# A decoder layer's last projection: eight feature blocks by seven quarter products, the residual through DRAM, one weight cast moved

## The chip, the core and the metric

The kernel runs on one core of a Trainium2 chip. The core has a matrix engine (TensorE, PE in the profile; PEld are its weight loads), VectorE (DVE), ScalarE (ACT), GpSimd (POOL) and SyncE (SP), which here issues the DMAs. Each engine works through its own instructions in order and waits on semaphores. The metric is the device time of one execution in microseconds. The kernel before took 1062.61 us (median of three runs, 1062.47 to 1064.94).

## What is computed

One decoder layer over 512 tokens of width 1024, all in float32. A token mixer (attention, pooling and a state-space scan) ends in a projection w_o that is added to the residual. The part that matters here comes after it:

```python
def rmsnorm(x, g):
    y = xf * lax.rsqrt(jnp.mean(xf * xf, axis=-1, keepdims=True) + NORM_EPS)
    return y * g

def conv_ffn(u, w_up, conv_w, conv_b, w_down):
    h = causal_dwconv(u @ w_up, conv_w, conv_b)      # 512 x 5632
    a, v = h[..., :D_FF], h[..., D_FF:]              # D_FF = 2816 = 22 x 128
    return (jax.nn.silu(a) * v) @ w_down             # 512 x 1024
...
x = x + merged @ w_o[i]
x = x + conv_ffn(rmsnorm(x, ln2_g[i]), ...)
return rmsnorm(x, final_g)
```

The last projection multiplies 512 x 2816 activations by the 2816 x 1024 matrix w_down. With features in 22 blocks of 128 (KF), tokens in four blocks of 128 and columns in two halves of 512, that is 22 x 4 x 2 = 176 block products.

## The kernel before

**A float32 product is three matmuls.** Each operand is split into a high part, rounded to the type that TensorE takes (float32r), and a low part, the rest. `mm3` (matmul at L221) adds high by high, high by low and low by high in one PSUM bank: over all feature blocks of a job first with the weight's high part, then high again, and only then with its low part.

**Weights come as jobs.** The program is a list of jobs, each with a piece of weights, mostly a tile of 128 partitions by 2048 elements (1 MB), and a body that issues its matmuls. The main loop gives each job n, before its body, a `prepare`: `low` of job n+1 (VectorE subtraction, L204), `cast` of job n+2 (ScalarE, two halves, L184), `fetch` of job n+3 (a DMA on SP, L174). Raw weights have two buffers, high parts three and low parts two, so a fetch waits until a low part has been taken, and a low part waits until TensorE has finished the job that had its buffer. The two halves of a cast are normally put in a list (`second`) and issued at the next calls of `step`, which also advances small pieces of other work (`running`).

**The order on TensorE, ScalarE, VectorE and GpSimd is that of the program text** (a schedule by hand). SP's order is found when the kernel is built, by a scheduler.

**The seam between w_o and up.** The w_o jobs run for token blocks 0 and 1, then 2 and 3, each with column half 0 and then 1. `wo_jobs` adds the result to the residual tiles X1 (L939), starts the norm with half 0 (`norm_early`: squares on ScalarE at L306, product with the gain on POOL at L330) and ends it with half 1 (`norm_late`, L306, then xg at L339, v, a root, and u at L347); the result is transposed on TensorE (`norm_turn`, L319) and split into uh and ul (L322, L323). For the last w_o job and the first up job `prepare` is called with `later=True` from the job's body, and returns a part that is run at a later place: for the last w_o job, after block 3's norm has been issued. An argument `now` says whether the cast is issued at once (last w_o job: yes) or with that part (first up job). The first two up jobs (`opening`, L1036) begin with the 256 tokens whose norm is done, and transpose blocks 2 and 3 between their products.

**The up projection.** 22 jobs of 256 columns; `up_evac` applies the convolution and gate (L1000, L1003, L1005, POOL at L1008) and `later` splits each of the 22 feature blocks in high and low (L1016, L1017), kept in ACTS.

**The down projection.** `down_jobs(0)` and `down_jobs(1)`, one per column half: six jobs each (four feature blocks a job, the last with two), 12 matmuls for each full job and token block, four accumulators. Results are added to X1 (L1078); half 0 starts the final norm, and half 1 ends it and stores the output (L1086). In half 1 the last two jobs run token block by token block, so that the norms follow one another.

Small tiles of 128 x 512 come from one pool of 54 slots (`T`); PSUM has four banks for `MM` and four for `SM`.

## Time and profile before

| what | value |
|---|---|
| median of three runs | 1062.61 us |
| profiled execution, time | 1064.09 us |
| its span, first to last instruction | 1062.2 us |
| mean granted TensorE clock | 0.995 |
| down projection on TensorE, 528 matmuls | 119.69 us |
| one 128x512 matmul in it | 0.2267 us |
| low part of a 128x2048 weight tile, VectorE | 2.29 us |
| cast of half of one, ScalarE | 1.04 us |
| bytes moved in the span | 115.50 MB |

The profile's page gives busy times of engines, the span in 40 slices, the chain of work that ended last, and groups of instructions with what ended the idle time before them. A row of a timeline has start, duration, engine, line, operation, output and inputs, and in brackets the idle time before and who ended it. Matmuls are pipelined, so their single durations (0.389 us) are longer than the step from one to the next; the step is the length of a stretch over its matmuls.

### The profile page before, as it was taken

The numbers are of one execution on the slowest core, as the hardware profiler recorded it, in microseconds if no ns is written. First come the engines' busy times: TensorE is split into PE (matmuls) and PEld (weight loads), VectorE is DVE, ScalarE is ACT, GpSimd is POOL, SyncE is SP. The second block draws the span as 40 slices with busy tenths as digits, with TensorE's granted clock in tenths as the row PEclk, the third lists the DMA queues.
The fourth block names the chain that finished last, engine by engine and source line by source line (L and its number), as shares of the span: only waits on it lengthen the run. The fifth ranks groups of instructions, "written<-read, shape, count | busy, mean of one in ns | idle before, by whom it ended". The sixth has DMA issues, their size and how long they took to land.

```text
span 1062.2 us, 13018 instructions
## 1 busy us (share of the span) xinstructions
PE 1045.9 (98%) x5268; PEld 874.4 (82%) x5268; DVE 576.8 (54%) x777; ACT 431.1 (41%) x698; POOL 135.1 (13%) x118
## 2 busy tenths in 40 slices
PE   8999999999999999999999999989999999999997
PEld 8878889888788887787888888888888888888885
DVE  5552523245667547667658766556656565532315
ACT  6343412232445633558536224534444444431311
POOL 1580000000000001100161500002111111110100
PEclk9999999999999999999999999989999999999999
DMA  7236233251221365442243337333232323232312
GB/s 237 79 115 179 82 100 107 72 140 50 83 80 60 83 166 158 110 129 81 80 111 119 119 97 263 119 118 101 95 104 81 118 80 119 80 119 69 110 60 79
DMA packets 116426, 115.50 MB, mean 109 GB/s; under 512 B 5235, under 2 KB 101302, under 8 KB 116367
## 3 DMA queue, kind: packets, MB, share of 16 engines
q1 hardware_dynamic: 116367, 114.68, 35.5%
q8 instruction: 41, 0.67, 0.3%
q14 instruction: 18, 0.15, 0.0%
HBM read 110.87 MB, written 2.22 MB: 106 GB/s over the span
## 4 chain that ended last, share of the span: by engine, by line
PE 91%; ACT 2%; issue 2%; DVE 2%; DMA 1%; POOL 0%; SPq 0%; DVEq 0%; ACTq 0%; POOLq 0%
PE pa L221 35%; PE pu L221 22%; PE pb L221 17%; PE pqk L221 9%; PE ps L512 1%; PE ppw L221 1%; PE po L551 1%; PE pt L539 1%; PE pu L1036 1%; ACT wh L184 1%; PE py L808 1%; DVE wl L204 1%; PE pyo L814 1%; DMA raw<-in_w_in_dram 1%; DMA raw<-in_ffn_w_up_dram 0%
## 5 line engine op out<-in xcount | busy, mean ns | idle before, releaser
L204 DVE TENSOR_TENSOR wl<-raw,wh 128x2048 fp32r<-128x2048 f32 (+3 forms) x94 | 219.2, 2333 | 137.9 <-PE pb L221 67.7
L184 ACT CAST wh<-raw 128x1024 fp32r<-128x1024 f32 (+2 forms) x186 | 187.2, 1025 | 109.6 <-PE pb L221 40.8
L221 PE MATMUL pa<-uh,wh 128*128 128x512 f32 x384 | 99.3, 400 | 0.3 <-ACT wh L184 0.3
L1003 DVE SCALAR_TENSOR_TENSOR hc<-pu,fcol,hc 128x510 f32<-128x510 f32 x88 | 65.9, 749 | 55.9 <-ACT hc L1000 54.3
L221 PE MATMUL pa<-ul,wh 128*128 128x512 f32 x384 | 95.0, 389 | 0.0
L221 PE MATMUL pa<-uh,wl 128*128 128x512 f32 x384 | 94.9, 389 | 0.0
L221 PEld LDWEIGHTS pa<-ul,wh 128*128 128x128 f32 x384 | 72.1, 188 | 15.3
L221 PEld LDWEIGHTS pa<-uh,wl 128*128 128x128 f32 x384 | 72.1, 188 | 15.0
L221 PE MATMUL pu<-ul,wh 128*128 128x512 f32 (+1 forms) x352 | 83.5, 379 | 0.0
L221 PE MATMUL pu<-uh,wl 128*128 128x512 f32 (+1 forms) x352 | 83.5, 379 | 0.0
L221 PE MATMUL pu<-uh,wh 128*128 128x512 f32 (+1 forms) x352 | 83.5, 379 | 0.0
L221 PEld LDWEIGHTS pa<-uh,wh 128*128 128x128 f32 x384 | 69.9, 188 | 16.5 <-issue 1.7
L221 PEld LDWEIGHTS pu<-uh,wl 128*128 128x128 f32 x352 | 64.2, 188 | 12.5
L221 PEld LDWEIGHTS pu<-ul,wh 128*128 128x128 f32 x352 | 64.2, 188 | 12.5
L221 PEld LDWEIGHTS pu<-uh,wh 128*128 128x128 f32 x352 | 64.1, 188 | 12.4
L1000 ACT ACTIVATE hc<-pu,fcol,fcol 128x512 f32<-128x512 f32 x40 | 31.2, 780 | 83.5 <-PE pu L221 83.5
L1008 POOL TENSOR_TENSOR hc<-hc 128x512 f32<-128x512 f32 x22 | 31.6, 1435 | 230.1 <-DVE hc L1003 188.1
L787 POOL TENSOR_TENSOR xd<-xc,dec 128x512 f32<-128x512 f32 x6 | 6.4, 1065 | 361.6 <-DVE xc L778 343.0
L533 ACT ACTIVATE sb<-sb,nm 128x128 f32<-128x128 f32 (+1 forms) x72 | 30.1, 419 | 46.9 <-DVE nm L530 33.2
L221 PE MATMUL pb<-wh,fh 128*128 128x512 f32 x176 | 47.7, 389 | 0.0
L221 PE MATMUL pb<-wl,fh 128*128 128x512 f32 x176 | 47.7, 389 | 0.0
L221 PE MATMUL pb<-wh,fl 128*128 128x512 f32 x176 | 47.7, 389 | 0.0
(273 smaller groups left out, 1601.8 us busy)
## 6 DMA issues: line engine op xcount, KB each, us to landing
raw<-in_w_in_dram SPq DMA_DIRECT2D x25, 1024.0 KB
raw<-in_ffn_w_up_dram SPq DMA_DIRECT2D x22, 1024.0 KB
raw<-in_w_in_dram SPq DMA_DIRECT2D x20, 512.0 KB
raw<-in_ffn_w_down_dram SPq DMA_DIRECT2D x10, 1024.0 KB
raw<-in_w_o_dram SPq DMA_DIRECT2D x8, 1024.0 KB
raw<-in_w_in_dram SPq DMA_DIRECT2D x6, 768.0 KB
raw<-in_w_b_dram SPq DMA_DIRECT2D x4, 1024.0 KB
al<-ad SPq DMA_DIRECT2D x16, 256.0 KB
```

The lines of the kernel that those rows point to most:

```text
L184: act.copy(job.high[:, :, o], job.raw[:, :, o])
L204: (eng or dve).tensor_tensor(l[:, :, o], job.raw[:, :, o], h[:, :, o].bitcast(F32), OP.subtract)
L221: pe.matmul(ps, l, r, start=first and n == 0, stop=last and n == total - 1)
L512: pe.matmul(pss[i][:, o:o + w * P], q[r, n * P:(n + 1) * P], k[r, kb * P:(kb + w) * P], start=True, stop=True)
L533: act.activation(sb[:, off:off + w * P], sb[:, off:off + w * P], AF.Exp, bias=nm[:, n, h:h + 1], accum_out=ls[:, n, h:h + 1])
L539: pe.transpose(pt[:, o:o + P], sb[:, o:o + P], eye)
L551: pe.matmul(po[DH * hh:DH * hh + DH, n * P:(n + 1) * P], V[g, kb + i][:, (2 * c + hh) * DH:(2 * c + hh + 1) * DH], probs[2 * c + hh, nb][: ...
L808: pe.matmul(py[DH * i:DH * i + DH, j * P:(j + 1) * P], xc[:, o:o + DH], als[j // 2][:, lo:lo + P], start=True, stop=True)
L814: pe.matmul(po[:, j * P:(j + 1) * P], prev[gi][:, j * P:(j + 1) * P], XS[10 + gi][:, cs], start=True, stop=True)
L1000: act.activation(t, ps, AF.Identity, bias=ff["c1"][:, ff["b"] + m:ff["b"] + m + 1], scale=fw(2, m))
L1003: dve.scalar_tensor_tensor(t[:, sh:], ps[:, :S - sh], fw(k, m), t[:, sh:], OP.mult, OP.add)
L1008: pool.tensor_tensor(a, a, t, OP.mult)
```

## The change

- **Seven products.** Of the 22 feature blocks the first eight (KS) are taken as four pairs. With tokens, features (even and odd blocks) and columns in halves, that part is a 2 x 2 by 2 x 2 product of quarters. It is computed by the scheme of seven products (Strassen's in Winograd's form) in place of eight, p1 to p7 of 24 matmuls each. `sums_of` forms the sums of activations in the up projection, `form` makes the differences of weights in place on VectorE, in buffers of one.raw, four.raw and in W. Four of the products go to PSUM banks of their own and are added to X1 by VectorE; p2, p4 and p3 share accumulators with the 14 other feature blocks, which `blocks_of` runs as before.
- **Order of the down jobs.** p2, four jobs of other blocks for half 0, p1, p5, p6, p7, p4, p3, four jobs for half 1.
- **The residual.** `put_x1` writes the eight X1 tiles to DRAM, `get_x1` reads them into one tile that takes the place of ul; W takes the place of uh.
- **The cast at the seam.** `prepare` has no `now`: with `later=True` low, cast and fetch are all in the part that is run later. For the last w_o job the cast moves behind block 3's norm; for the first up job nothing moves.

```diff
 DFF = 2816
 KF = DFF // P
+KS = 8
 C_Q, C_K, C_V = 0, AW, 2 * AW
 C_POOL = 3 * AW
...
     def fetch(job, cuts=1):
+        if job.load:
+            job.load()
+            return
...
     def cast(job, cuts=1, spread=False):
         w = job.c // cuts
+        if job.form:
+            job.raw = job.form()
         job.high = whp.tile([P, job.k, job.c], F32R, name="wh", tag="wh")
...
@@ -252,7 +260,7 @@
             wh, wl = ws
             mm3(acc[tb][:, :c], lambda k: wh[:, k - k0, :], lambda k: wl[:, k - k0, :],
                 lambda k: xh(k, tb), lambda k: xl(k, tb), range(k0, k1),
-                k0 == 0, k1 == nk, flip=True)
+                k0 == 0 and tb not in opened, k1 == nk and tb not in keep, flip=True)
...
@@ -260,7 +268,8 @@
             def body(ws, n=n, k0=k0, k1=k1):
                 if n == 0:
                     for tb in blocks:
-                        acc[tb] = (mk or MM)("pb")
+                        if tb not in opened:
+                            acc[tb] = (mk or MM)("pb")
...
                 for tb in blocks:
                     for a in (held if late else [(k0, k1, ws)]):
                         use(*a, tb)
-                    if k1 == nk:
+                    if k1 == nk and tb not in keep:
                         evac(tb, acc[tb])
                     if tb % 2:
                         step()
...
+    def put_x1():
+        nxt["x1"] = dram.tile([4, 2, P, S], F32, name="x1d")
+        for tb, h in X1:
+            sp.dma_start(nxt["x1"][tb, h], X1[tb, h])
+    def get_x1():
+        back = upool.tile([P, KD, S], F32, name="x1b", tag="ul")
+        for h in range(2):
+            for tb in range(4):
+                X1[tb, h] = back[:, 2 * tb + h, :]
+                sp.dma_start(X1[tb, h], nxt["x1"][tb, h])
...
@@ -1010,14 +1031,157 @@
         def later():
             yield
             k = m - KF
+            if k >= KS or k % 2:
+                h, l = T("fh", F32R), T("fl", F32R)
+                act.copy(h, a)
+                dve.tensor_sub(l, a, h.bitcast(F32))
+                ACTS[k] = (h, l)
+                if k < KS:
+                    yield
+                    for _ in sums_of(k // 2, HC[k - 1], a):
+                        yield
+                return
             if k == 0:
-                wide.extend(ypool.tile([P, 4, S], F32R, name=n, tag="xs") for n in ("fh", "fl"))
-            h, l = (t[:, k, :] for t in wide) if k < 4 else (T("fh", F32R), T("fl", F32R))
-            act.copy(h, a)
-            dve.tensor_sub(l, a, h.bitcast(F32))
-            ACTS[k] = (h, l)
+                wide.extend(ypool.tile([P, 4, S], F32R, name=n, tag="xs") for n in ("sh", "sl"))
+            t = T("f0", F32R)
+            act.copy(t[:, :256], a[:, :256])
+            dve.tensor_sub(t[:, 256:], a[:, :256], t[:, :256].bitcast(F32))
+            FS[0, k // 2] = (t[:, :256], t[:, 256:])
         running.append(later())
+    FS = {}
+    def sums_of(p, f0, f1):
+        lo, hi = slice(0, 256), slice(256, S)
+        sa, sb = T("sa"), T("sb")
+        dve.tensor_tensor(sa[:, lo], f0[:, hi], f1[:, hi], OP.add)
+        dve.tensor_tensor(sa[:, hi], sa[:, lo], f0[:, lo], OP.subtract)
+        dve.tensor_tensor(sb[:, lo], f0[:, lo], f0[:, hi], OP.subtract)
+        dve.tensor_tensor(sb[:, hi], f1[:, lo], sa[:, hi], OP.subtract)
+        yield
+        ah, al = (t[:, p, :] for t in wide)
+        bh, bl = T("sbh", F32R), T("sbl", F32R)
+        act.copy(ah, sa)
+        act.copy(bh, sb)
+        yield
+        dve.tensor_sub(al, sa, ah.bitcast(F32))
+        dve.tensor_sub(bl, sb, bh.bitcast(F32))
+        FS[1, p], FS[2, p] = (ah[:, lo], al[:, lo]), (ah[:, hi], al[:, hi])
+        FS[3, p], FS[4, p] = (bh[:, lo], bl[:, lo]), (bh[:, hi], bl[:, hi])
+    def down():
+        n2 = KS // 2
+        quarter = lambda two, h: w_down[:KS * P, h * S:(h + 1) * S].rearrange(
+            "(k two p) c -> two p k c", two=2, p=P)[two]
+        W, acc, rs = {}, {0: {}, 1: {}}, {}
+        def load(at, two, h):
+            def fn():
+                if not W:
+                    W["u"] = upool.tile([P, KD, S], F32, name="w3", tag="uh")
+                W[at] = W["u"][:, 4 * at:4 * at + 4, :]
+                sp.dma_start(W[at], quarter(two, h))
+            return fn
+        def diff(out, a, b):
+            dve.tensor_tensor(out, a, b, OP.subtract)
+            return out
+        def product(ps, ws, parts, first, last):
+            wh, wl = ws
+            mm3(ps, lambda k: wh[:, k, :], lambda k: wl[:, k, :], lambda k: parts[k][0],
+                lambda k: parts[k][1], range(n2), first, last, flip=True)
+        def first_half(i):
+            return [[t[:, i * P:(i + 1) * P] for t in FS[0, p]] for p in range(n2)]
+        def second_half(tb):
+            return [[t[:, tb * P:(tb + 1) * P] for t in ACTS[2 * p + 1]] for p in range(n2)]
+        def sums(j, i):
+            return [[t[:, i * P:(i + 1) * P] for t in FS[j, p]] for p in range(n2)]
+        def add(tb, h, what):
+            dve.tensor_tensor(X1[tb, h], X1[tb, h], what, OP.add)
+        def early(tb):
+            yield
+            fin[tb] = norm_early(X1[tb, 0], fin["g"])
+        def job(parts, use, form=None, ld=None):
+            def body(ws):
+                for i in range(2):
+                    use(i, ws)
+                    step()
+            j = Job(parts, n2, S, body)
+            j.form, j.load = form, ld
+            return j
+        def p2(i, ws):
+            acc[0][i] = MM("pb")
+            product(acc[0][i], ws, second_half(i), True, False)
+        def p1(i, ws):
+            ps = SM("p1")
+            product(ps, ws, first_half(i), True, True)
+            add(i, 0, ps)
+            rs[i] = T("r1")
+            act.copy(rs[i], ps)
+            running.append(early(i))
+        def p5(i, ws):
+            ps = SM("p5")
+            product(ps, ws, sums(1, i), True, True)
+            add(i, 1, ps)
+            add(2 + i, 1, ps)
+        def p6(i, ws):
+            ps = SM("p6")
+            product(ps, ws, sums(2, i), True, True)
+            dve.tensor_tensor(rs[i], rs[i], ps, OP.add)
+        def p7(i, ws):
+            ps = SM("p7")
+            product(ps, ws, sums(3, i), True, True)
+            r3 = T("r3")
+            dve.tensor_tensor(r3, rs[i], ps, OP.add)
+            def rest():
+                yield
+                add(i, 1, rs[i])
+                add(2 + i, 0, r3)
+                yield
+                add(2 + i, 1, r3)
+            running.append(rest())
+        def p4(i, ws):
+            product(acc[0][2 + i], ws, second_half(2 + i), False, True)
+            add(2 + i, 0, acc[0][2 + i])
+            running.append(after(2, early(2 + i)))
+        def p3(i, ws):
+            acc[1][i] = SM("pb")
+            product(acc[1][i], ws, sums(4, i), True, False)
+        one = job([quarter(0, 0)], p1)
+        five = job([], p5, lambda: diff(one.raw, W[0], one.raw), load(0, 0, 1))
+        six = job([], p6, lambda: diff(one.raw, W[1], one.raw), load(1, 1, 1))
+        seven = job([], p7, lambda: diff(W[0], W[1], W[0]), lambda: None)
+        four = job([quarter(1, 0)], p4, lambda: diff(four.raw, four.raw, one.raw))
+        yield job([quarter(1, 0)], p2)
+        yield from blocks_of(0, acc[0], (0, 1), (2, 3))
+        for j in (one, five, six, seven, four, job([quarter(1, 1)], p3)):
+            yield j
+        yield from blocks_of(1, acc[1], (0, 1), ())
...
             def body(ws):
                 uh2, ul2 = nxt["uh"], nxt["ul"]
-                low = job.prepare(later=True, now=False) if half == 0 else None
+                low = job.prepare(later=True) if half == 0 else None
                 if half == 0:
...
-    def down_jobs(h):
+    def blocks_of(h, acc, opened, keep):
         def evac(tb, ps):
             t = X1[tb, h]
             dve.tensor_tensor(t, t, ps, OP.add)
             if h == 0:
-                fin[tb] = norm_early(t, fin["g"])
                 return
...
-        return jobs_b(lambda k0, k1: [wsrc(w_down, k0, k1, h * S, h * S + S)], S,
-                      lambda k, tb: ACTS[k][0][:, tb * P:(tb + 1) * P],
-                      lambda k, tb: ACTS[k][1][:, tb * P:(tb + 1) * P], KF, evac,
-                      mk=(MM, SM)[h], tail=2 if h else 0)
+        return jobs_b(lambda k0, k1: [wsrc(w_down, KS + k0, KS + k1, h * S, h * S + S)], S,
+                      lambda k, tb: ACTS[KS + k][0][:, tb * P:(tb + 1) * P],
+                      lambda k, tb: ACTS[KS + k][1][:, tb * P:(tb + 1) * P], KF - KS, evac,
+                      mk=(MM, SM)[h], tail=2 if h else 0, acc=acc, opened=opened, keep=keep)
...
-        yield from up_jobs()
+        for i, job in enumerate(up_jobs()):
+            yield job
+            if i == 3:
+                yield Call(put_x1)
         yield Call(lambda: fin.setdefault("g", grow(final_g)))
         yield Call(finish)
-        yield from down_jobs(0)
-        yield from down_jobs(1)
+        yield Call(get_x1)
+        yield from down()
...
         if n >= 2:
-            def prepare(n=n, later=False, now=True):
-                def high():
-                    if n + 2 < len(weights):
-                        cast(weights[n + 2], 2, spread=not later)
+            def prepare(n=n, later=False):
                 def rest():
                     if n + 1 < len(weights):
                         low(weights[n + 1])
-                    if not now or not later:
-                        high()
+                    if n + 2 < len(weights):
+                        cast(weights[n + 2], 2, spread=not later)
                     if n + 3 < len(weights):
                         fetch(weights[n + 3])
                 if later:
-                    if now:
-                        high()
                     return rest
                 rest()
```

More of the change, by code (lines that the diff above doesn't have):

```diff
@@ L78, in __init__ @@
         self.late = self.short = False
+        self.load = self.form = None
 @with_exitstack
@@ L243, in jobs_b @@
     def jobs_b(parts_of, c, xh, xl, nk, evac, kstep=4, mk=None, blocks=range(4), tail=0,
-               turn_over=False):
-        acc = {}
+               turn_over=False, acc=None, opened=(), keep=()):
+        acc = {} if acc is None else acc
         starts = list(range(0, nk, kstep))
```

## The prediction

> **What bounds the kernel.** I read the page's busy times first, then the chain of waits in order of time, then tables of windows, then the timelines of single engines around the two places that the diff touches.
>
> ```profile
> PE 1045.9 (98%) x5268; PEld 874.4 (82%) x5268; DVE 576.8 (54%) x777; ACT 431.1 (41%) x698; POOL 135.1 (13%) x118
> ...
> 681.24 5.20 DMA raw<-in_ffn_w_up_dram
> 686.54 2.00 ACT wh L184 x2
> 688.54 0.63 ACT junk L306 x2
> 690.33 1.00 DVE u L347 x2
> ...
> 692.88 2.21 DVE wl L204
> 695.13 8.18 PE pu L1036 x48
> ...
> 706.09 229.15 PE pu L221 x1056
> 935.24 119.69 PE pb L221 x528
> ```
>
> TensorE is the bound: 98% busy, and in the down projection the chain is 528 matmuls in 119.69 us, 0.2267 us each, without a gap. Only one place near the edit leaves TensorE waiting: between the last w_o job and the up projection the chain runs through a DMA, ScalarE and VectorE. The windows show its price (columns: stretch, length, then PE busy (count), granted clock, DMA share, GB/s):
>
> ```profile
> 366.00:372.00 6.00, 5.66 (x36) 1.00 0.11 25
> ...
> 689.30:695.10 5.80, 1.09 (x9) 0.84 0.23 67
> 695.10:698.50 3.40, 3.37 (x15) 0.50 0.79 249
> 698.50:701.00 2.50, 2.50 (x17) 0.69 0.44 142
> ```
>
> TensorE idles 5.80 - 1.09 = 4.7 us, and then loses 3.40 x 0.50 + 2.50 x 0.31 = 2.5 us to a lower clock: 7.2 us in all. An idle 0.34 us, in the first row, left the clock alone.
>
> **Edit 1, the cast behind the second norm.** Before, ScalarE's cast of the second up job (L184) is issued at the start of the last w_o job, so it stands in ScalarE's queue ahead of the norm's squares (L306) and waits for its weights until 686.54. Block 2's residual add ended at 683.49 (682.80 + 0.69), so its squares, which began at 688.45, could have begun at 683.52: 4.93 us earlier. From there I keep the durations of the rows. Squares to both u: 2.88 us, 686.4. Residual add of block 3: 686.32 to 687.0; xg and v to 687.9; then the low part of the first up job, 2.28 us: 690.15 in place of 695.08. TensorE has meanwhile done two products (to 689.2) and eight transposes (0.87 us, row of the chain), so it waits about 0.1 us, and the clock has no idle stretch to fall in. The moved cast now begins about 688.1, after its weights (686.54), and ends at 690.1; the second half's first product needs it at about 692.2. Behind it on ScalarE are the copies of the transposes, free at 690.2. The fetch of the third up job goes out with the low part, 690.2 in place of 695.14, and lands about 695.3. So TensorE's stretch from 685.09 to 705.81 shrinks to six products of 16 x 0.12 us (the step between 256-wide weight loads at 705.81, 706.77, 707.73 is 0.96 for eight) plus two groups of transposes: 11.5 + 1.7, with small waits 13.9 in place of 20.7. **-6.8 us**; bounds -3 (the clock still falls and half the idle time stays) and -7.2.
>
> [...]
>
> **Edit 2, seven products.** Four pairs of blocks: 8 x 4 x 2 x 3 = 192 matmuls become 7 x 24 = 168. 24 x 0.2267 = **-5.44 us**, if TensorE stays fed. The six products after the first block group are jobs of 5.44 us where every other job is 10.88 us, and each still needs a 2.29-us low part and two 1.04-us casts. New on VectorE in that stretch are four weight differences (128x2048, f32; nearest row the low part, 2.29) and 18 additions of 0.68 (row of L1078). These rows give the durations:
>
> ```profile
> 940.69 2.28 DVE L204 TENSOR_TENSOR wl<-raw,wh 128x2048 fp32r<-128x2048 f32 x1
> ...
> 993.48 0.68 DVE L1078 TENSOR_TENSOR x<-x,pb 128x512 f32<-128x512 f32 x1
> ...
> 916.04 1.59 POOL L1008 TENSOR_TENSOR hc<-hc 128x512 f32<-128x512 f32 x1 [4.09 <-DVE hc L1003]
> 916.40 3.38 DVE L204 TENSOR_TENSOR wl<-raw,wh 128x2048 fp32r<-128x2048 f32 x1
> ```
>
> From the start of the short fourth block job (t = 0) to the first long job after the products, VectorE has seven low parts (16.0), four differences (9.2), two evictions and 18 additions (13.6): 38.8 us, plus waits, against seven TensorE jobs of 5.44 = 38.1. It is no longer hidden. I walked its queue in program order:
> - the difference for the sixth product ends at 11.5. The first product's two additions follow, and then the small v of the early norm waits for ScalarE, which has two half casts and the squares ahead: VectorE goes on at 14.95.
> - the difference for the seventh ends at 19.7; its two casts end at 22.6 with squares between them; TensorE wants it at 21.8. Wait **0.95**.
> - the difference for the fourth ends at 27.75, its casts at 29.8; TensorE, now at 28.15, waits **1.75**.
> - the next product's weights can be fetched only when that difference has read its buffer, 27.75; with the 5.3 us that fetches take here (681.24 to 686.54) and two casts they are ready at 35.1, just in time (35.35).
> - VectorE then has a low part and six additions to do. POOL's multiplication xg (1.30) of blocks 2 and 3 falls beside them: in the row at 916.40 the low part took 3.38 and ended 2.15 after POOL did, so it stood still. Twice 1.3 us brings the low part of the first long job from 43.95 to 46.5. TensorE wants it after eight matmuls, at 42.6. Wait **4.0**.
> - one more: the first product of the projection is a 5.44-us job in place of 10.88. The next low part ends at 942.97 and is wanted 32 matmuls after 935.1, at 942.35. Wait **0.7**.
>
> Waits 7.4 in all, so the stretch is 119.7 - 5.4 + 7.4: **+2.0 us**. Bounds: -4.7 (VectorE keeps pace, only the 0.7 stays) and +7 (each of the eleven wide subtractions at 2.76, their mean in the up projection, 11 x 0.47 = 5.2 more). I take the walked value, since POOL has only four instructions there.
>
> [...]
>
> **Edit 3, sums in the up projection.** Per pair four half-width VectorE operations (between 0.15 and 0.69 by the rows of one and of 512 columns, say 0.42), two casts of 0.62, two subtractions of 0.69, less one half-width split: some 2.7 us of VectorE, 11 in all. VectorE is busy 134.4 of 229 us there, and results wait in four PSUM banks while two are filled: nothing on the path. Without that cover, up to 11 us.
>
> **Edit 4, the residual.** Eight writes and eight reads of 256 KB, and 2 MB more weights (two quarters twice). SP issues what is ready, not what the program has first: the load of the final gain, written after all up jobs, goes out at 692.73.
>
> ```profile
> 692.73 0.35 SPq L312 DMA_DIRECT2D grow<-in_final_g_dram  x1
> 695.14 203.31 SPq L174 DMA_DIRECT2D raw<-in_ffn_w_up_dram  x20
> ...
> 948.37 2.00 ACT L184 CAST wh<-raw 128x1024 fp32r<-128x1024 f32 x2 [6.43 <-DMA raw<-in_ffn_w_down_dram]
> ```
>
> So I expect the writes between 648 and 691, each as its block is done, not behind the fourth up job. Most fall behind the fetch at 681.24, and 256 KB (a quarter of 5.2 us) still leaves the cast its slack of 2 us. The reads wait on SP for the last up matmul, with the two quarters for the differences; behind them is the fetch of the fourth down job. 5.2 MB in all at the 244 GB/s seen from 632 to 650 is 21.5 us, so it lands at 21.5 after the stage's start, its low part ends at 26, wanted at 30: **0**; bounds 0 and +1.3.
>
> **Sum.** -6.8 + 2.0 + 0 + 0 = -4.8. The profiled execution had a span of 1062.2 and a time of 1064.09; against that 1059.3, against the median of 1062.61, which lies nearer the span: **1057.8 us**, own range 1054 to 1061.
>
> **Rivals.**
> 1. VectorE keeps up (the additions slip into gaps, v does not wait): -6.8 - 4.7 = -11.5, 1051.1. For: low parts have a lead of almost a job. Against: 38.8 of work for 38.1. Chance 0.14.
> 2. The residual's writes do come ahead of the up fetch, so that half of edit 1's gain goes: -3.4 + 2.0, 1061.2. It needs 1 MB ahead of the fetch at 681.24; only 0.5 MB becomes ready just before it. This is also the case in which the write is not where the program puts it. Chance 0.14.
> 3. Slower: in the product stretch VectorE stays locked against POOL, as at 916.40, for each wide subtraction: 11 x 1.09 = 12 us, 1069.8. It decides from about 0.73 us each (8 us). Against: POOL has 5 us of work in that stretch. Chance 0.18.
>
> The forecast has 0.54. About 0.3% (3.2 us) can be told from no change. Faster: 0.54 x 0.85 + 0.14 + a little of rival 2, 0.61; same: 0.54 x 0.15 + most of rival 2, 0.20; slower: 0.19. The range 1051.5 to 1064 leaves out most of rival 3 and the edge of rival 1.
>
> **What would show it.** Right: squares of block 2 directly behind its add, no low clock in that stretch, the first 512-wide up matmul some 7 us earlier; the chain leaving TensorE for VectorE and ScalarE casts inside the products; a wait of some us on the low part of the first long job behind them. Wrong: an unbroken TensorE there (rival 1), a DMA wait ahead of the moved cast that TensorE feels (rival 2), or wide subtractions of 3 us (rival 3).

## The result, and the profile after

| | before | changed |
|---|---|---|
| median | 1063.05 us (6 runs, 1062.47 to 1064.94) | 1059.82 us (6 runs, 1058.91 to 1060.20) |
| ratio to before, 95% interval | | 0.9967 (0.9954 to 0.998) |
| profiled execution, time | 1064.09 us | 1058.91 us |
| its span | 1062.2 us | 1057.1 us |
| mean granted TensorE clock of it | 0.995 | 0.999 |
| seam: first up matmul (L1036, now L1200) to the first at L221 (now L228) | 20.61 us | 14.30 us |
| up projection, 1056 matmuls | 229.15 us | 229.26 us |
| down projection, first to last matmul | 119.83 us | 121.30 us |

The changed kernel is 0.33% faster: 3.2 us by the medians, 2.1 to 4.9 by the interval. The two profiled executions are 5.2 us apart. Their spans, 5.1 us apart, add up from their parts: -6.3 at the seam, +0.1 and +1.5 in the two projections, and -0.4 in what lies before and behind. The pair overstates the gain, because the profile of before is 1 us above its median and that of the changed kernel is the shortest of its six; the runs on the clock, below, show what the other five probably have more.

The page's busy line of the changed kernel (engine, busy us, share of the span, instructions):

```profile
PE 1040.9 (98%) x5244; PEld 867.0 (82%) x5244; DVE 613.4 (58%) x824; ACT 441.1 (42%) x714; POOL 135.5 (13%) x118
```

TensorE has 24 matmuls less and is busy 5.0 us less, and VectorE has 36.6 us more to do. Where that work falls decides. The chain of waits of the changed kernel, through the seam and on (start, duration, engine, output, line):

```profile
682.58 0.70 DVE x L960
683.31 0.73 ACT junk L315 x2
...
686.84 0.73 ACT junk L315 x2
687.89 1.99 ACT wh L191 x2
690.02 6.78 DMA raw<-in_ffn_w_up_dram
696.87 2.00 ACT wh L191 x2
698.87 0.49 ACT uh L331
699.40 229.42 PE pu L228 x1056
928.82 5.45 PE pb L228 x24
934.31 2.25 DVE wl L211
...
1009.35 0.69 DVE x1b L1112
1010.03 3.31 DVE wl L211
1013.39 36.59 PE pb L228 x160
```

The squares of block 2 (L315, 683.31) now stand directly behind its residual add, and the cast (L191) comes at 687.89, behind the squares of block 3. The first up matmul at L228 starts at 699.40 in place of 705.93. (The prediction calls it the first 512-wide one. It is still 256 wide, the start of the second 256 tokens; the 512-wide ones begin at 711.03 in place of 717.45, 6.4 us earlier.) What ends the seam now is the third up job: fetched at 690.02, landed 6.78 us later. Behind the products the chain leaves TensorE for VectorE and comes back only at 1013.39. The windows of the seam, TensorE's rows (stretch, length, PE busy (count), granted clock, DMA share, GB/s):

```profile
683.30:688.00 4.70, 4.70 (x34) 1.00 0.73 249
688.00:692.00 4.00, 3.96 (x34) 1.00 0.60 196
692.00:699.40 7.40, 6.82 (x58) 1.00 0.80 265
```

Of the 4.7 us without a matmul, 0.6 are left, and the clock is full throughout. In the kernel before those 4.7 us were two waits, with eight transposes between them:

```profile
691.02 1.08 PE L319 MATMUL uT<-eye,u 128*128 128x128 f32 x8 [1.72 <-DVE u L347]
695.13 3.79 PE L1036 MATMUL pu<-uh,wl 128*128 128x256 f32 x16 [3.03 <-DVE wl L204]
```

The timeline of TensorE of the changed kernel in the product stretch, all rows that waited (the bracket has the idle time before, and who ended it):

```profile
990.78 1.20 PE L228 MATMUL p<-wh,sbh 128*128 128x512 f32 x4 [1.00 <-ACT wh L191]
993.44 1.19 PE L228 MATMUL p<-wl,sbh 128*128 128x512 f32 x4 [0.56 <-DVE wl L211]
997.75 1.20 PE L228 MATMUL pb<-wh,fh 128*128 128x512 f32 x4 [0.39 <-ACT wh L191]
1000.08 1.20 PE L228 MATMUL pb<-wl,fh 128*128 128x512 f32 x4 [0.22 <-DVE wl L211]
1013.39 0.96 PE L228 MATMUL pb<-wl,fh 128*128 128x512 f32 x3 [2.13 <-DVE wl L211]
```

With the 0.53 us at the second down job (936.61) these are all. Since single matmuls overlap, each costs about 0.16 us more than its bracket when counted from one matmul's start to the next: 0.70, then 1.16 + 0.72 at the seventh product, 0.54 + 0.38 at the fourth, 2.29 at the first long job. And the timelines of VectorE and POOL ahead of that last one:

```profile
1005.65 2.99 DVE L1112 TENSOR_TENSOR x1b<-x1b,r 128x512 f32<-128x512 f32 x3
1005.81 1.68 POOL L339 TENSOR_TENSOR xg<-x1b,grow 128x512 f32<-128x512 f32 x1 [23.34 <-DVE x1b L1112]
1008.74 0.69 DVE L1112 TENSOR_TENSOR x1b<-x1b,pb 128x512 f32<-128x512 f32 x1
1009.57 1.61 POOL L339 TENSOR_TENSOR xg<-x1b,grow 128x512 f32<-128x512 f32 x1 [2.08 <-DVE x1b L1112]
1009.95 3.38 DVE L211 TENSOR_TENSOR wl<-raw,wh 128x2048 fp32r<-128x2048 f32 x1
```

Three additions with both inputs in SBUF take 2.99 us and the low part 3.38, in place of 1.89 and 2.28 (both measured without POOL, below). Each has an xg of POOL inside it. Last, SP's timeline, to where the residual's writes went:

```profile
648.36 3.06 SPq L948 DMA_DIRECT2D x1d<-x  x2
659.24 4.96 SPq L948 DMA_DIRECT2D x1d<-x  x2
674.45 1.96 SPq L948 DMA_DIRECT2D x1d<-x  x2
683.30 3.85 SPq L948 DMA_DIRECT2D x1d<-x  x2
```

Two tiles at a time, each as its block is done, although the program issues them behind the fourth up job.

### The profile page after: what moved, and what is told of

Read it like the earlier page. It is cut to its first block, busy times and chain, and to the rows that moved or that the text cites. A ratio compares the mean times of both kernels' runs of the same rounds, so it can differ in the third digit from the quotient of the medians.

```text
span 1057.1 us, 13071 instructions
## 1 busy us (share of the span) xinstructions
PE 1040.9 (98%) x5244; PEld 867.0 (82%) x5244; DVE 613.4 (58%) x824; ACT 441.1 (42%) x714; POOL 135.5 (13%) x118
## 4 chain that ended last, share of the span: by engine, by line
PE 86%; DVE 5%; ACT 3%; issue 3%; DMA 2%; POOL 1%; SPq 0%; DVEq 0%; ACTq 0%; POOLq 0%
PE pa L228 33%; PE pu L228 22%; PE pb L228 15%; PE pqk L228 9%; DVE wl L211 2%; ACT wh L191 1%; PE ps L521 1%; PE ppw L228 1%; PE po L560 1%; PE pt L548 1%; PE py L817 1%; DVE raw L1093 1%; DMA raw<-in_ffn_w_up_dram 1%; PE pyo L823 1%; DVE x1b L1112 1%
## 5 line engine op out<-in xcount | busy, mean ns | idle before, releaser
L191 ACT CAST wh<-raw 128x1024 fp32r<-128x1024 f32 (+3 forms) x190 | 191.4, 1025 | 103.4 <-PE pa L228 32.9
L228 PE MATMUL pa<-uh,wh 128*128 128x512 f32 x384 | 99.3, 400 | 0.3 <-ACT wh L191 0.3
L228 PE MATMUL pa<-uh,wl 128*128 128x512 f32 x384 | 95.0, 389 | 0.1
L228 PE MATMUL pa<-ul,wh 128*128 128x512 f32 x384 | 95.0, 389 | 0.0
L228 PEld LDWEIGHTS pa<-uh,wl 128*128 128x128 f32 x384 | 72.0, 188 | 15.4 <-DVE wl L211 0.5
L228 PEld LDWEIGHTS pa<-ul,wh 128*128 128x128 f32 x384 | 72.1, 188 | 15.3
L228 PE MATMUL pu<-uh,wh 128*128 128x512 f32 (+1 forms) x352 | 83.7, 380 | 0.6 <-ACT uh L331 0.6
L228 PE MATMUL pu<-uh,wl 128*128 128x512 f32 (+1 forms) x352 | 83.5, 379 | 0.0
L228 PE MATMUL pu<-ul,wh 128*128 128x512 f32 (+1 forms) x352 | 83.5, 379 | 0.0
L228 PEld LDWEIGHTS pa<-uh,wh 128*128 128x128 f32 x384 | 69.9, 188 | 16.5 <-issue 1.7
L228 PEld LDWEIGHTS pu<-uh,wh 128*128 128x128 f32 x352 | 64.1, 188 | 13.2 <-ACT uh L331 0.8
L228 PEld LDWEIGHTS pu<-uh,wl 128*128 128x128 f32 x352 | 64.2, 188 | 12.5
L228 PEld LDWEIGHTS pu<-ul,wh 128*128 128x128 f32 x352 | 64.2, 188 | 12.5
L919 DVE TENSOR_TENSOR sg<-sg,pa 128x512 f32<-128x512 f32 x24 | 16.1, 684 | 41.7 <-PE pa L228 41.6
L228 PE MATMUL pb<-wl,fh 128*128 128x512 f32 x128 | 35.2, 392 | 2.9 <-DVE wl L211 2.9
L228 PE MATMUL pqk<-uh,wh 128*128 128x512 f32 x144 | 36.7, 397 | 0.0
```

The costliest lines, as they stand in the source:

```text
L191: act.copy(job.high[:, :, o], job.raw[:, :, o])
L228: pe.matmul(ps, l, r, start=first and n == 0, stop=last and n == total - 1)
L919: dve.tensor_tensor(s, s, ps, OP.mult)
```

## The experiments

The theory: the seam gives nearly 7 us, the products as written cost some 2 to 3 because VectorE has more to do than TensorE, and the residual's round trip costs nothing. The first rival was that the seam gives less (the writes take part of it) and the products cost less; the second, that POOL and not the amount of VectorE's work makes the waits. Ratios are to the kernel before on the same chip.

**The cast alone.** The kernel before, with `now` taken out, so that the cast moves and nothing else changes.

```diff
-                low = job.prepare(later=True, now=False) if half == 0 else None
+                low = job.prepare(later=True) if half == 0 else None
...
-                    if not now or not later:
-                        high()
+                    if n + 2 < len(weights):
+                        cast(weights[n + 2], 2, spread=not later)
...
-                    if now:
-                        high()
```

> The kernel before with the moved cast alone (no products, no residual traffic). My theory, that the two gains add and the cast is worth what the trace of the changed kernel shows at the seam (first 512-wide up matmul 6.3 us earlier after the w_o start is taken out): 6.0 us below the kernel before, 5.0 to 6.8, so faster than the full change. Rival A, that the profile of before was an execution with an unusually long clock loss at the seam: only 3 to 4.5 us below in the median, though its own profile shows no low clock between 685 and 700. Rival B, that the cast is worth nothing without the rest: within 1 us of before.

Measured: 1056.65 us (1056.42 to 1057.08), ratio 0.9937 (0.9924 to 0.9949), so 6.7 us faster than before, and 3 us faster than the whole change by the ratios. Its chain of waits:

```profile
698.64 229.15 PE pu L221 x1056
927.79 119.69 PE pb L221 x528
```

It is TensorE alone, with the down projection of before. The seam took 13.56 us. This one move is worth more than the whole change, so the other parts together lose.

**The products alone.** The changed kernel, with `now` and the place of the cast put back as before.

```diff
-                low = job.prepare(later=True) if half == 0 else None
+                low = job.prepare(later=True, now=False) if half == 0 else None
...
+                    if now:
+                        high()
```

> The changed kernel with the cast at the seam put back to the start of the last w_o job. My theory: the seam costs again what it cost before, and the seven products with the residual's round trip cost about 1.5 us net, so 1 to 3 us above the kernel before. Rival A (short clock loss at the seam in most executions): still 1 to 3 us above, since both have the seam. Rival C, that the products do pay in most executions and the seam does not: 1 to 4 us below.

Measured: 1066.69 us (1065.45 to 1068.46), ratio 1.0035 (1.0023 to 1.0048): slower, by 3.2 us as the medians stand on that chip and by 3.7 as the ratio has it, somewhat more than the 1 to 3 expected. The two parts add up: 0.9937 x 1.0035 = 0.9972, against 0.9967 for the change. Its down projection took 122.89 us, 1.6 more than that of the changed kernel's profile, with the same waits. The difference is in the granted clock. TensorE's windows of this kernel, from ahead of the long wait:

```profile
1015.00:1018.30 3.30, 1.19 (x7) 1.00 0.01 2
1018.30:1020.00 1.70, 1.70 (x5) 0.60 0.29 27
1020.00:1022.00 2.00, 2.00 (x7) 0.50 1.00 390
```

and of the changed kernel at the same place:

```profile
1010.00:1013.40 3.40, 1.27 (x7) 1.00 0.01 2
1013.40:1015.00 1.60, 1.60 (x7) 1.00 0.34 20
1015.00:1017.00 2.00, 2.00 (x11) 1.00 0.91 340
```

The idle time is the same, 2.1 us. In one execution the clock falls to half for about 3.4 us behind it (worked out from the windows, the next of which, 1022 to 1024, has 0.99), in the other it stays at 1.00: 7 matmuls in 2 us, or 11.

**Does the clock change from one execution to the next?** The changed kernel profiled twice more, and the products alone once more, nothing edited.

> The changed kernel unaltered, for a second profile. Its first profile had a mean clock of 0.999 and the shortest span of its six executions, 1057.1; the other five had 0.996 to 0.997 and 1057.8 to 1058.4. My theory: in most executions the clock falls after the wait at the first long job, as in the profile with the cast put back (half clock for 3.4 us after 2.1 us of idle TensorE), so the 160 matmuls behind it take about 38.2 in place of 36.6 us and the span is 1058 to 1059. Rival: the spread has another place, the stage before w_o for one, and the 160 matmuls take 36.6 us again.

> The changed kernel once more, unaltered, for a third profile. Two profiles had no low clock behind the wait at the first long job, though five of six timed executions had spans 0.7 to 1.3 us above the first profile's. If the clock is the cause of that spread, a profile with a span of 1058 or more shows half clock for some 3 us behind that wait and a down projection of 122.5 to 123 us; if not, the down projection is 121.3 again and the extra time lies ahead of w_o.

> The products with the cast put back, unaltered, for a second profile. The first had half clock for 3.4 us behind the wait at the first long job and a down projection of 122.89 us. If the fall of the clock hangs on where the wait happens to lie, the second may lack it: 121.3 us; if it belongs to this kernel, 122.9 again.

| profile | time | idle at that wait | clock behind it | down projection |
|---|---|---|---|---|
| changed kernel, first | 1058.91 | 2.13 | 1.00 | 121.30 |
| changed kernel, second | 1058.46 | 2.12 | 1.00 | 121.28 |
| changed kernel, third | 1059.02 | 2.12 | 0.50 for about 3.4 us | 122.95 |
| products alone, first | 1065.45 | 2.11 | 0.50 for about 3.4 us | 122.89 |
| products alone, second | 1065.69 | 2.13 | 0.50 for about 3.4 us | 122.92 |

TensorE's windows of the third profile of the changed kernel:

```profile
1009.00:1013.00 4.00, 1.88 (x8) 0.96 0.08 10
1013.00:1014.50 1.50, 1.50 (x5) 0.50 0.85 205
1014.50:1016.50 2.00, 2.00 (x7) 0.59 1.05 410
1016.50:1018.50 2.00, 2.00 (x10) 1.00 0.58 211
```

So it comes and goes with the execution, and it is worth 1.6 us.

The length of the wait does not decide it alone: the changed kernel had 2.12 us in both its second and its third profile, and the clock stayed at 1.00 behind one and was 0.50 behind the other. At the seam of the kernel before, too, it was 0.50 behind the waits of 1.72 and 3.03 us. What decides it was not shown; no run moved such a wait on purpose.

Of the six timed runs of the changed kernel the profiled one has a mean clock of 0.999, the other five 0.996 or 0.997; the third profile above has 0.997. That the five lost their clock at this very wait fits (3.4 us at half clock lower the mean over 1058 us by 0.0016) and was not seen, since they have no trace.

**The round trip alone**, in the kernel before, and then on top of the moved cast.

```diff
+    def put_x1():
+        nxt["x1"] = dram.tile([4, 2, P, S], F32, name="x1d")
...
-        yield from up_jobs()
+        for i, job in enumerate(up_jobs()):
+            yield job
+            if i == 3:
+                yield Call(put_x1)
...
+        yield Call(get_x1)
```

> The kernel before with the residual written to DRAM and read back and nothing else. My theory: hidden, within 0.8 us of the kernel before; the writes go out one by one between 648 and 692, the reads when the last up matmul is done. Rival E, that the round trip costs part of what the products save: 1.5 to 4 us above the kernel before, by a weight cast that waits longer for its DMA at the seam or in the second down job.

> The kernel with the moved cast alone, plus the residual's round trip, without the products. My theory: the eight writes go out between 648 and 692 ahead of the third up job's fetch, which lands 6 to 7 us after its issue in place of 5.3; the cast behind it and the copies of the last transposes come later and TensorE waits for them, 14.1 to 14.4 us at the seam in place of 13.56; 0.4 to 1.0 us above the kernel with the cast alone. Rival: the round trip is hidden here as it is in the kernel before (0.3 us, inside the noise), and the longer seam of the changed kernel has another cause: within 0.3 us.

Measured: in the kernel before 1063.77 us, ratio 1.0002 (0.9993 to 1.0011), with the writes at the same times as in the changed kernel (648.16 to 683.10). On top of the moved cast 1056.84 us, ratio 0.9944 (0.993 to 0.9957), against 1056.65 and 0.9937 without: no difference that can be told. The seam took 13.55 us, not the 14.1 to 14.4 that the expectation took from the changed kernel's profile. There the third up job's fetch landed late (6.78 us), in the second profile likewise (seam 14.18), but in the third the seam was 13.54. The late landing is not a fixed price of the writes.

**The work put off.** In the changed kernel, six additions of product seven and the four early norms (`early`) are issued some steps later, beside the long jobs behind the products, where VectorE has room. Nothing is taken away.

```diff
-            running.append(early(i))
+            running.append(after(11, early(i)))
...
-            running.append(rest())
+            running.append(after(5, rest()))
...
-            running.append(after(2, early(2 + i)))
+            running.append(after(5, early(2 + i)))
```

> The changed kernel with six additions and the four early norms of the product stretch issued later, in the long jobs behind it; nothing else moves, the same work in all. My theory, VectorE is the bound in the stretch: the waits at the low part of the first long job (2.3 us) and at the seventh product (1.9) vanish, about 1 us at the fourth product stays; 4 to 5.5 us below the changed kernel, 7 to 9 below the kernel before. Rival D, that the stretch waits for its weights' DMAs (the buffer that p3 and the long jobs are fetched into): the waits stay, within 1.5 us of the changed kernel.

Measured: 1053.81 us (1052.92 to 1054.54), ratio 0.9909 (0.9895 to 0.9922): 9.65 us faster than before, 2.8 faster than the moved cast alone on the same chip, some 6 faster than the change, and more than the 7 to 9 below before that were expected. The down projection took 117.39 us, and no wait on TensorE was above 0.53 us in it. So the seven products do pay, by about half of their 5.4 us, once the work that nobody waits for stands where VectorE is not the bound. This run does not separate VectorE's work from POOL's: the xg of blocks 2 and 3 moved out of the stretch with their norms, to 1015.82 and 1019.00 us. Those of blocks 0 and 1 ran at 978.30, as early as in the change.

**POOL or the amount of work?** The changed kernel, with the xg of blocks 2 and 3 computed by VectorE, and their early norms three steps later. VectorE has more to do than in the change.

```diff
-    def norm_early(t, g):
+    def norm_early(t, g, eng=None):
-        pool.tensor_tensor(xg, t, g[:, :S], OP.mult)
+        (eng or pool).tensor_tensor(xg, t, g[:, :S], OP.mult)
-            fin[tb] = norm_early(X1[tb, 0], fin["g"])
+            fin[tb] = norm_early(X1[tb, 0], fin["g"], dve if tb > 1 else None)
-            running.append(after(2, early(2 + i)))
+            running.append(after(5, early(2 + i)))
```

> The changed kernel with one thing taken away from the stretch: POOL's two multiplications for the early norm of blocks 2 and 3 are done by VectorE in the second long job behind the products; all additions stay where they are. My theory, VectorE stands still beside POOL: the three additions after the fourth product take 2.07 in place of 2.99 us, the low part of the first long job 2.29 in place of 3.31, TensorE's wait there falls from 2.3 to about 0.4 us and the clock has no idle stretch left to fall in; 1.8 to 3.5 us below the changed kernel. Rival: those instructions are long for another reason (DMA traffic, the source buffer), so they keep their lengths, within 0.8 us of the changed kernel.

Measured: 1056.50 us (1055.18 to 1057.01), ratio 0.9929 (0.9916 to 0.9942), 4 us faster than the change by the ratios and 3.3 by the medians, where 1.8 to 3.5 were expected. VectorE's and TensorE's timelines, for the rows shown above of the change:

```profile
1005.92 1.89 DVE L1112 TENSOR_TENSOR x1b<-x1b,r 128x512 f32<-128x512 f32 x3
1009.12 2.28 DVE L211 TENSOR_TENSOR wl<-raw,wh 128x2048 fp32r<-128x2048 f32 x1
1011.46 1.21 PE L228 MATMUL pb<-wl,fh 128*128 128x512 f32 x4
```

The same three additions and the same low part are 1.1 us shorter each, and the last row has no bracket: the wait of 2.1 us is gone, and the clock is 1.00. The down projection took 119.11 us, 2.2 less than in the change's first profile, and these two rows make 2 x 1.1 us of that. It is also 0.7 below the 119.83 of the kernel before, though VectorE has more to do than in the change. Two things were changed at once, POOL's work moved to VectorE and the norms put off by three steps. Either takes POOL's xg away from these rows, so they show that the instructions took 1.89 and 2.28 us with no xg beside them; which of the two earned the rest was not tried apart.

**The early norms of blocks 0 and 1 put off alone.** The rival that only VectorE's wait for v matters: the first of the three edits of the work put off.

```diff
-            running.append(early(i))
+            running.append(after(11, early(i)))
```

> The changed kernel with only the early norm's squares and small v of blocks 0 and 1 issued in the first long job behind the products. My theory: VectorE's queue no longer stands behind ScalarE for v (3.06 and 0.62 us before v in the changed kernel); the low parts of the sixth and seventh product come about 1 us earlier, the waits at the seventh product (1.9 us) fall to about 0.5, the later ones stay for the most part; 1 to 2.5 us below the changed kernel. Rival: v waits in time that VectorE has free anyway, because the low part behind it waits for the same casts; within 0.6 us.

Measured: 1059.22 us (1058.01 to 1061.60), ratio 0.9959 (0.9947 to 0.9971), not to be told from the change. Its timelines of POOL, VectorE and TensorE show why:

```profile
1003.61 4.08 DVE L1112 TENSOR_TENSOR x1b<-x1b,r 128x512 f32<-128x512 f32 x3
1003.83 3.32 POOL L339 TENSOR_TENSOR xg<-x1b,grow 128x512 f32<-128x512 f32 x2 [71.62 <-issue]
1012.42 1.19 PE L228 MATMUL pb<-wl,fh 128*128 128x512 f32 x4 [3.39 <-DVE v L338]
```

All four xg now fall into the same stretch. The three additions take 4.08 us beside them, and TensorE's wait there grows from 2.13 to 3.39 us (the bracket names v, which ended within 0.1 us of the low part that TensorE waits for: 1009.01 and 3.36 us). The clock stayed full behind it: 1.00 in the windows from 1012.40 to 1016.50. What was won at the seventh product is lost again at the first long job.

**The product p2 between the fifth and the sixth**, on top of the work put off (with the early norms of blocks 0 and 1 now 13 steps later), so that TensorE has 5.4 us of other work between VectorE's differences; then the same with all four xg on VectorE.

```diff
-            acc[0][i] = MM("pb")
-            product(acc[0][i], ws, second_half(i), True, False)
+            product(acc[0][i], ws, second_half(i), False, True)
+            add(i, 0, acc[0][i])
...
-        yield job([quarter(1, 0)], p2)
-        yield from blocks_of(0, acc[0], (0, 1), (2, 3))
-        for j in (one, five, six, seven, four, job([quarter(1, 1)], p3)):
+        yield from blocks_of(0, acc[0], (), (0, 1, 2, 3))
+        for j in (one, five, job([quarter(1, 0)], p2), six, seven, four, job([quarter(1, 1)], p3)):
```

> The kernel with the deferred additions and norms, and in addition the product p2 moved from the start of the projection to a place between the fifth and the sixth product; the work is the same. My theory: p2 needs no weight difference, so among the products it gives VectorE 5.4 us of TensorE time for 2.3 of its own, and the projection begins with a long job, so the 0.7 us wait at the second job goes as well. Of the 3.0 us of waits that the deferred kernel still has (117.3 against 504 x 0.2267 = 114.3), 1.5 to 2.7 go: 1.5 to 3 us below the deferred kernel. Rival: the waits are set by the fetch and cast of each differenced weight, whatever runs between, so within 0.7 us of the deferred kernel.

> The kernel with p2 between the fifth and the sixth product, and in addition all four early multiplications of the final norm on VectorE, behind the products, in place of POOL. In the profile of the kernel without this, POOL's multiplications of blocks 0 and 1 fell on the low part of the seventh product (3.29 us, TensorE waited 0.97). My theory: that low part takes 2.29 again and the down projection falls from 116.85 to about 115.9 us; 0.5 to 1.5 us below that kernel, about 10.5 below the kernel before. Rival: four more operations of 0.69 on VectorE cost elsewhere what they save: no difference beyond 0.5.

Measured: 1054.28 us, ratio 0.9908 (0.9895 to 0.9921), no better than the work put off, where 1.5 to 3 were expected. The rows show POOL again, now on the seventh product:

```profile
986.79 2.55 POOL L339 TENSOR_TENSOR xg<-x1b,grow 128x512 f32<-128x512 f32 x2 [53.72 <-issue]
988.20 3.29 DVE L211 TENSOR_TENSOR wl<-w,wh 128x2048 fp32r<-128x2048 f32 x1 [0.95 <-ACT wh L191]
991.54 1.20 PE L228 MATMUL p<-wl,sbh 128*128 128x512 f32 x4 [0.97 <-DVE wl L211]
```

With all four xg on VectorE: 1052.91 us (1052.18 to 1053.51), ratio 0.9904 (0.9891 to 0.9918), 10.1 us faster than before. Its down projection is the shortest, 115.85 us, and only two waits are left, 0.37 and 0.22 us at the fourth product. By their times the last three kernels cannot be told apart; by the profile this one has the least idle TensorE.

## Why the prediction was right, and where it was off

It had 1057.8 us; the median is 1059.82, 2.0 us above it and inside the range.

**Edit 1 was right, in mechanism and size.** It had -6.8; the moved cast alone measured -6.7 by the ratio and -7.05 at the seam, the changed kernel's profile -6.3. Squares of block 2 directly behind the add, predicted at 683.52, came at 683.31; the first up matmul of the second 256 tokens (699.40), 7 us earlier by the text, came 6.5 earlier. The clock stayed full (1.00 in the three windows above), as the missing idle stretch had it. One small term was missing: the third up job's fetch was to land 5.1 us after 690.2, and took 6.78 in this profile, which held TensorE for some 0.6 us. In the third profile of the changed kernel it did not.

**Edit 2 was right in sign and cause, and too small.** It had +2.0 for the stage; the profile has +1.5, and executions in which the clock falls +3.1; the products alone cost 3.2 to 3.7 us. The sum of the waits, 7.4, came near the loss in part by luck: the stage took 121.30 us, and 504 matmuls at 0.2267 are 114.26, so 7.0 were lost, but only 5.8 of them in the four waits below. The other 1.2 had no term; most of it lies directly behind the waits, where the first four matmuls take 1.03 us in place of 0.91. The places were less good:

| wait | predicted | measured, first profile |
|---|---|---|
| second down job | 0.7 | 0.70 |
| seventh product | 0.95 | 1.88 |
| fourth product | 1.75 | 0.92 |
| first long job behind the products | 4.0 | 2.29 |

At the seventh product VectorE stood still longer than walked: it waited 3.06 us for v of the first early norm and 0.62 for the second, where the walk had 2.1 for the first and named none for the second. At the last wait, counted from the end of the sixth product's difference, the low part was to end 35.0 us later and TensorE to want it at 31.1; it ended at 34.1 and was wanted at 31.9. What the two xg add to VectorE's instructions, 2 x 1.3 us in the walk, measured 2 x 1.1 us.

**The step that failed is the clock.** The sum took all waits of edit 2 at full clock, the one of 4.0 us too. It read the seam's 4.7 idle us as one stretch; the rows of the kernel before, shown above, have two, 1.72 and 3.03 us, and the clock was 0.50 behind them, so it had fallen behind shorter waits than 4.7 us in the very profile that the prediction had. The wait became 2.1 us, and the clock fell behind it in three of five profiles, at 1.6 us each. With it, -6.8 + 2.0 + 1.6 is -3.2, which is the median's difference; without it, the first profile's 1058.91 lies 0.4 from the 1059.3 predicted for a profiled execution. Part of this agreement is chance, since seam and products each missed by some tenths.

**Edit 3 and edit 4 cost nothing, as said.** The up projection went from 229.15 to 229.26 us with the additional VectorE work in it, and the round trip alone had a ratio of 1.0002. The place of the writes was right, too: they went out as the blocks were done, between 648 and 687.

**The rivals.** VectorE keeping up (1051.1) fell: the products alone are slower. The writes ahead of the up fetch (1061.2) fell as a mechanism, though the changed kernel's median lies near its figure: the seam kept its gain with the round trip added. POOL beside every wide subtraction (1069.8) fell: one of the eleven was longer (3.38 us, besides the three additions of 2.99), where POOL was at work, and the others took 2.28 or 2.29, as POOL has only four instructions there.

**POOL beside VectorE, and the clock.** With an xg of POOL beside them, three additions with both inputs in SBUF took 2.99 us in place of 1.89, and a low part 3.38 in place of 2.28; an addition from PSUM took 0.68 us at 979.72 with an xg beside it from 979.93, and 0.68 at 1005.05 with none. These rows show the times and not the cause. The clock was 0.50 for about 3.4 us behind a wait of 2.1 us in three profiles, and stayed at 1.00 behind such a wait in two and behind one of 3.39 us in another kernel's.

**What stays open.** What decides whether the clock falls behind a wait of some 2 or 3 us is not known from these runs. Whether the remaining 1.6 us of waits in the best kernel (115.85 less 114.26) can be had was not tried.

## What to carry to other kernels

Fewer matmuls are a gain only as long as the engines that prepare their operands have time left in that very stretch: count their work against TensorE's there, not over the span, and put off every addition that nobody waits for. Where VectorE is the bound and its work gets longer beside a small operation of GpSimd (1.1 us here, beside an xg of 1.61 to 1.68), let VectorE do it itself, or put it where VectorE has room: with the xg of two blocks moved to VectorE and put off, the kernel became 4 us faster. And a cast that waits for its weights should not stand in an engine's queue ahead of work that is ready: with this one moved alone, the kernel became 6.7 us faster.

## What the runs showed that was not expected

- Behind a wait of TensorE of 2.1 us its clock was 0.50 for about 3.4 us in three of five profiles and 1.00 in the other two, and behind a wait of 3.39 us (the early norms of blocks 0 and 1 put off) it was 1.00.
- POOL's xg were not equally long either: in the changed kernel 1.27 us while VectorE mostly waited (two in 2.54 from 979.93), and 1.61 and 1.68 beside the low part and the three additions; with the norms of blocks 0 and 1 put off, four of them with VectorE busy throughout took 3.32 and 4.94 a pair. With p2 between the fifth and the sixth product, a pair took 2.55 although the low part beside it took 3.29.
- The fetch of 1 MB behind the seam, issued at about 690, is not equally fast from one execution to the next: with the residual's writes ahead of it, the cast that waits for it began between 5.0 and 6.9 us after its issue (nine profiles), and 5.3 us after it without them. The median landing of its kind is 5.1.
